# Taking the low-part subtraction of every fourth weight tile from VectorE to GpSimd in a decoder-block kernel

## The chip, the cores and the metric

The kernel runs on one core of one Trainium2 chip. The metric is the device time of one execution in microseconds (us). The engines are called as in the profile: PE is TensorE, PEld its weight load, ACT ScalarE, DVE VectorE, POOL GpSimd and SP SyncE, whose queue issues nearly all DMAs.

## What is computed

One layer of a decoder block for 256 tokens of width 2048, in float32: a norm, one wide projection, a gated mixer and a block attention beside each other, an output projection, and an MLP with a squared ReLU.

```python
h = rmsnorm(x, ln_mix[l])
z = h @ w_in[l]
uv, qkv, gates = jnp.split(z, [2 * A_WIDTH, 2 * A_WIDTH + 3 * B_WIDTH], axis=-1)
y_a = spatial_gating_mixer(uv, a_v_gain[l], a_spatial[l], a_spatial_bias[l]) @ w_proj_a[l]
q, k, v = jnp.split(qkv, 3, axis=-1)
y_b = moba_mixer(q, k, v, rel_bias) @ w_proj_b[l]
g_a, g_b = jnp.split(gates, 2, axis=-1)
merged = jax.nn.sigmoid(g_a) * y_a + jax.nn.sigmoid(g_b) * y_b
x = x + merged @ w_out[l]
h = rmsnorm(x, ln_mlp[l])
x = x + jnp.square(jax.nn.relu(h @ w_up[l])) @ w_down[l]
return rmsnorm(x, ln_final)
```

The block of keys is as long as the sequence, so the attention is plain causal attention with a bias by distance (`rel_bias`).

## The kernel before, in words

Each weight matrix is cut into tiles of 512 rows by 512 columns, 1 MB each, 288 in all, used one after the other in a fixed order: 48 for keys, queries and values (in PSUM tiles `kt`, `qt`, `v`), 16 each for `gb`, `pb`, `gv`, `u`, `pa`, `ga` and `wo`, then four rounds of 16 for `up` and 16 for `dn`, the last four of them named `last`. Tiles are counted from 0 here. Four tiles in a row make one chunk of 512 output columns.

`WeightStream` brings a tile in and splits it. `load` (line 56) puts one DMA on SP's queue into a buffer `wraw`, of which there are four. `split` rounds the tile into a high part `whi` on ACT (line 72) and takes `wlo = wraw - whi` on DVE (line 73). There are three buffers for `whi` and three for `wlo`, so tile n is split into the buffers that PE has read for tile n-3. `get` issues loads five tiles ahead and splits two tiles ahead. A load into a `wraw` buffer waits until ACT and DVE have read the tile that lay there, four tiles before. The first six tiles are split in pieces; tile 3 is split in two halves of 128x1024.

For each weight block PE makes three products: high activations by `whi`, high by `wlo`, low by `whi`. In `rows` (lines 141 to 143) that is 24 matmuls of 512 columns for one tile; in `cols` (line 158) 48 matmuls of 256 columns in groups of four, the high activations by `whi` first, then the low ones by `whi`, then `wlo`.

Other work is issued between weight tiles by `tick`: the first norm (`sq`, sums of squares by three DVE additions on lines 236, 238 and 239; `ssqp`, a product on line 243; `rs_*`; then `rb1p`, line 223), the attention heads (scores `sc`, softmax in `l`, transposes `ptp` on line 316), and `bias_rows`. That makes a table of biases: a product `rvp` (line 280), a copy to `rv` on DVE (line 281), a memset of its end (line 282), and a DMA of 2048 rows of 1 KB each to DRAM, `rv_d` (line 285). `load_bias` reads it back in pieces `bt` (line 292), the first of which the first softmax needs. SP's queue is served in order, so weight loads issued behind `rv_d` follow it.

POOL makes the identity at the start and masks four small tiles `ws` (line 423). A scheduler that works with its own durations orders each engine's instructions at build time; what is issued in a program's order above may stand elsewhere in an engine's queue.

Of the kernel before, what the change touches and what calls it, by code (L numbers as in the profile page):

```python
# [12 lines left out]
F32 = mybir.dt.float32  # L13
F32R = mybir.dt.float32r
AF = mybir.ActivationFunctionType
ALU = mybir.AluOpType
AX = mybir.AxisListType

P = 128
D = 2048  # L20
T = 256
NT = T // P
KT = D // P
# [5 lines left out]
EPS = 1e-6  # L29
NEG = -1e30  # L30
SCALE = P ** -0.5
CH = 512
KG = 4
# [1 line left out]


class WeightStream:
    """Weights in tiles of KG*128 rows by CH columns, laid out as in_tiles() does, each split exactly into two float32r parts:
    w = hi + lo. Loads and splits are issued ahead of the products that use them."""

    def __init__(self, nc, pool, chunks, ahead=2, loads_ahead=5):
        self.nc, self.pool = nc, pool
# [17 lines left out]
    def split(self, pieces=None, between=None):  # L60
        j = self.n_split
        t = self.raw.pop(j)
        if j == len(self.tiles) - 1 and self.spare:
            hi, lo = self.spare
        else:
            hi = self.pool.tile([P, KG, CH], F32R, tag="whi", name=f"whi{j}", bufs=3)
            lo = self.pool.tile([P, KG, CH], F32R, tag="wlo", name=f"wlo{j}", bufs=3)
        for a, b in pieces or (((0, 2), (2, 4)) if j < 6 else ((0, KG),)):
            if between:
                between(a, b)  # L70
            s = slice(a, b)
            self.nc.scalar.activation(hi[:, s], t[:, s], AF.Copy)  # L72
            self.nc.vector.tensor_tensor(lo[:, s], t[:, s], hi[:, s].bitcast(F32), ALU.subtract)  # L73
        self.parts[j] = (hi, lo)
        self.n_split += 1

# [11 lines left out]
def block_kernel(ctx, tc, x, x_t, ln_mix, w_in, v_gain, w_sp, b_sp, w_pa, w_pb, w_out, rel_bias,  # L88
# [23 lines left out]
        chunks += [(w_up, 0, b * D + c * CH) for c in range(4)]  # L112
        chunks += [(w_down, b * D, c * CH) for c in range(4)]

# [1 line left out]
    tasks = deque()  # L116

    def tick(limit=2):
# [10 lines left out]
    stream = WeightStream(nc, wpool, chunks)  # L129

    def rows(acts, name):
        """[tokens, CH] = acts.T @ W over 2048 rows, both token tiles."""
        ps = psum.tile([P, NT, CH], F32, tag="mm", name=name, bufs=2)
        for i in range(KT // KG):
            hi, lo = stream.get()
            for kk in range(KG):
                k = i * KG + kk
                ah, al = acts(k)
                for t in range(NT):
                    s = slice(t * P, (t + 1) * P)  # L140
                    nc.tensor.matmul(ps[:, t], ah[:, s], hi[:, kk], start=k == 0, stop=False)  # L141
                    nc.tensor.matmul(ps[:, t], ah[:, s], lo[:, kk], start=False, stop=False)  # L142
                    nc.tensor.matmul(ps[:, t], al[:, s], hi[:, kk], start=False, stop=k == KT - 1)  # L143
            if i < KT // KG - 1:
                tick()
        return ps

    def cols(acts, name):
        """[CH as 4 x 128, tokens] = W.T @ acts over 2048 rows."""
        ps = psum.tile([P, CH // P, T], F32, tag="mm", name=name, bufs=2)  # L150
        for i in range(KT // KG):
            hi, lo = stream.get()
            for kk in range(KG):
                k = i * KG + kk
                ah, al = acts(k)
                for j, (w, a) in enumerate(((hi, ah), (hi, al), (lo, ah))):
                    for n in range(CH // P):
                        nc.tensor.matmul(ps[:, n], w[:, kk, n * P : (n + 1) * P], a,  # L158
                                         start=k == 0 and j == 0 and n % 2 == 0,
                                         stop=k == KT - 1 and j == 2, skip_group_check=True)  # L160
            if i < KT // KG - 1:
                tick()
        return ps

# [1 line left out]
    ident = const.tile([P, P], F32, name="ident")  # L166
    make_identity(nc, ident)
    ones = const.tile([P, P], F32, name="ones")
# [17 lines left out]
    first = [((0, 1), (1, 2), (2, 3), (3, 4))] * 2 + [((0, 2), (2, 4))] * 2  # L186
# [4 lines left out]
    hh = hold.tile([P, KT, T], F32R, tag="h", name="hh", bufs=2)  # L191
# [10 lines left out]
        split_x(k)  # L202

    def rsqrt(dst, s, n, scale=1.0):
        """dst = (scale * s + EPS) ** -0.5, the table's root refined by a Newton step."""
        v = const.tile([P, n], F32, tag="rs_v", name="rs_v", bufs=2)
        y = const.tile([P, n], F32, tag="rs_y", name="rs_y", bufs=2)
        q = const.tile([P, n], F32, tag="rs_q", name="rs_q", bufs=2)
        nc.vector.tensor_scalar(v, s, scale, EPS, op0=ALU.mult, op1=ALU.add)
        nc.scalar.activation(y, v, AF.Sqrt)  # L210
        nc.vector.reciprocal(y, y)
        nc.vector.tensor_mul(q, y, y)
        nc.vector.tensor_mul(q, q, v)
        nc.vector.tensor_scalar(q, q, -0.5, 1.5, op0=ALU.mult, op1=ALU.add)
        nc.vector.tensor_mul(dst, y, q)

    def row_of(r, name):
        """r [token, 2] on every partition as a row [*, 256]."""
        ps = psum.tile([P, T], F32, tag="tp", name=name + "p", bufs=2)
        for t in range(NT):  # L220
            dg = const.tile([P, P], F32, tag="diag", name="dg", bufs=2)
            nc.vector.tensor_scalar(dg, ident, r[:, t : t + 1], None, op0=ALU.mult)
            nc.tensor.matmul(ps[:, t * P : (t + 1) * P], ones, dg, start=True, stop=True)
        rb = const.tile([P, T], F32, tag="rb", name=name, bufs=2)
        nc.vector.tensor_copy(rb, ps)
        return rb
# [22 lines left out]
    tasks.append(first_norm())  # L249

    def split_t(dst_h, dst_l, k0, src):
        """Two transposed blocks [128, 2, 256] in PSUM -> hi and lo parts of k0, k0 + 1."""
        nc.scalar.activation(dst_h[:, k0 : k0 + 2], src, AF.Copy)
        nc.vector.tensor_tensor(dst_l[:, k0 : k0 + 2], src, dst_h[:, k0 : k0 + 2].bitcast(F32),
                                ALU.subtract)

    def transpose_pair(src, k, name):
        """Blocks k, k + 1 (of 128 columns) of src [tokens, ...] -> PSUM [128, 2, 256]."""
        tp = psum.tile([P, 2, T], F32, tag="tp", name=name, bufs=2)
        for a in range(2):  # L260
            for t in range(NT):
                nc.tensor.transpose(tp[:, a, t * P : (t + 1) * P],
                                    src[:, t, (k + a) * P : (k + a + 1) * P], ident)
        return tp

# [1 line left out]
    bh = bl = None  # L267
    with tc.tile_pool(name="attn", bufs=1) as at:
        rv = at.tile([HEADS, RV], F32, tag="pt", name="rv", bufs=2)
# [53 lines left out]
            nc.scalar.activation(bh[:, h], pv, AF.Copy)  # L323
            nc.vector.tensor_tensor(bl[:, h], pv, bh[:, h].bitcast(F32), ALU.subtract)

        hacts = lambda k: (hh[:, k], hl[:, k])  # noqa: E731

        def scale_cols(ps, name):
            dst = at.tile([P, 4, T], F32, tag=name[:2], name=name, bufs=2)
# [6 lines left out]
        for c in range(4):  # L336
# [11 lines left out]
            ps = rows(hacts, f"v{c}")  # L348
# [4 lines left out]
                tasks.append(head(c, j, qt, kt, vt, bt))  # L353
            tick()

# [1 line left out]
        m = hold.tile([P, NT, D], F32, tag="m", name="m", bufs=1)  # L357
        for c in range(4):
            ps = rows(hacts, f"gb{c}")
# [4 lines left out]
        drain()  # L364

    with tc.tile_pool(name="gmlp", bufs=1) as gp:
# [1 line left out]
        for c in range(4):  # L368
            ps = rows(lambda k: (bh[:, k], bl[:, k]), f"pb{c}")
            for t in range(NT):  # L370
                s = m[:, t, c * CH : (c + 1) * CH]
                nc.vector.tensor_tensor(s, s, ps[:, t], ALU.mult)

# [1 line left out]
        gain = gp.tile([P, GROUPS], F32, name="gain")  # L375
        nc.sync.dma_start(gain, v_gain)
        gv = gp.tile([P, NT, D], F32, tag="gv", name="gv", bufs=1)
# [62 lines left out]
            for t in range(NT):  # L440
                nc.scalar.activation(pa[:, t, c * CH : (c + 1) * CH], ps[:, t], AF.Copy)

# [1 line left out]
        mh = ab.tile([P, KT, T], F32R, tag="ab", name="mh", bufs=2)  # L444
        ml = ab.tile([P, KT, T], F32R, tag="ab", name="ml", bufs=2)

# [13 lines left out]
                nc.vector.tensor_tensor(m[:, t, s], m[:, t, s], g[:, t], ALU.add)  # L460
            tasks.append(merged(c))

# [1 line left out]
    lnp = const.tile([P, KT], F32, name="lnp")  # L464
    nc.sync.dma_start(lnp, ln_mlp)
    x1 = hold.tile([P, NT, D], F32, tag="m", name="x1", bufs=1)
# [7 lines left out]
    r2 = const.tile([P, NT], F32, name="r2")  # L474

    def add_rows(ps, t, s, sums=None):
        """x1 += ps in columns s of token tile t; sums gets the sum of the squares."""
        xs = x1[:, t, s]
        nc.vector.tensor_tensor(xs, xs, ps, ALU.add)
        if sums is not None:  # L480
            jk = const.tile([P, CH], F32, tag="junk", name="jk", bufs=2)
            nc.scalar.activation(jk[:, : s.stop - s.start], xs, AF.Square, accum_out=sums)
# [24 lines left out]

    ab_open.close()

# [1 line left out]
    mlp = ctx.enter_context(tc.tile_pool(name="mlp", bufs=1))  # L511
    lnf = mlp.tile([P, D], F32, name="lnf")
    nc.sync.dma_start(lnf, bass.AP(tensor=ln_final.tensor, offset=ln_final.offset,
# [1 line left out]
    for b in range(DFF // D):  # L515
        hid = []
        for c in range(4):
# [10 lines left out]
                nc.scalar.activation(q, v, AF.Square)  # L528
                nc.vector.tensor_tensor(tl[:, s], q, th[:, s].bitcast(F32), ALU.subtract)
            hid.append((th, tl))  # L530
        acts = lambda k: (hid[k // 4][0][:, k % 4], hid[k // 4][1][:, k % 4])  # noqa: E731
        last = b == DFF // D - 1
        for c in range(3 if last else 4):
            ps = rows(acts, f"dn{b}_{c}")
# [5 lines left out]
                else:  # L540
                    add_rows(ps[:, t], t, s)

# [1 line left out]
    spare = [hold.tile([P, KG, CH], F32R, tag="h", name=f"spare{i}", bufs=2) for i in range(2)]  # L544
    stream.spare = tuple(spare)
    out_v = out.rearrange("(t p) d -> t p d", p=P)
# [42 lines left out]


def in_tiles(w):
    """[rows, cols] as [row tile, column tile, 128, KG, CH]: each weight tile in one piece."""
    r, c = w.shape
    return np.asarray(w).reshape(r // (KG * P), KG, P, c // CH, CH).transpose(0, 3, 2, 1, 4)


def _onehot():
    """Which bucket a distance of 255 - m falls in, for m < 256; the rest is masked."""
    n = np.arange(256)
    half = BUCKETS // 2  # L600
    large = half + (np.log(np.maximum(n, 1).astype(np.float32) / np.float32(half))
# [45 lines left out]
```

## Time and profile before

| | |
|---|---|
| runs, median | 1664.79 us (two runs: 1663.89 and 1665.68) |
| span of the profiled execution, first to last instruction | 1662.5 us |
| median less span, taken as what lies around it | 2.3 us |
| PE busy | 1651.6 us, 99% |
| DVE busy | 850.9 us, 51% |
| ACT busy | 688.8 us, 41% |
| POOL busy | 4.3 us |
| mean granted PE clock | 0.998 |
| DMA | 317.16 MB, mean 191 GB/s |

The page gives the span of the profiled execution and no other time for it, so its own time is read as the span and the 2.3 us around it. A row of a timeline is start, duration, engine, line, operation, names; in brackets stands the idle time of the engine before it and what ended it.

### The profile page before, as it was taken

To read this page: it belongs to the slowest core of one execution; us is meant where nothing else is said; L and a number is where in the kernel's file an instruction comes from. 1 tells how busy PE (TensorE), PEld (TensorE's weight loads), DVE (VectorE), ACT (ScalarE), POOL (GpSimd) and SP (SyncE) were. 2 spreads that over 40 slices of the span, in tenths; PEclk is the share of its full clock that TensorE was granted. 3 is DMA by queue.
4 is the path that set the end of the run, shared out by engine and by line. 5 is a ranking of instruction groups with operands and counts; after the bars stand their busy time and mean duration, and the time that the engine had idled before them with its cause. 6 is when DMAs were issued, how large, how long until landed. Compare 5 with 4: busy or idle time off the path is not lost.

```text
span 1662.5 us, 22670 instructions
## 1 busy us (share of the span) xinstructions
PE 1651.6 (99%) x9988; PEld 1483.7 (89%) x9988; DVE 850.9 (51%) x726; ACT 688.8 (41%) x614; POOL 4.3 (0%) x11
## 2 busy tenths in 40 slices
PE   9999999999999999999999999999999999999997
PEld 9899999888888899888888999889988998899986
DVE  7545544544445555544555555444545455445554
ACT  7444343443334443434444444334443443334432
POOL 0000000000000000000000000000000000000000
PEclk9999999999999999999999999999999999999999
DMA  9855444465555554555465554555555555555551
GB/s 317 254 193 187 165 178 170 159 223 185 200 192 189 192 199 169 184 191 202 178 234 189 210 178 178 202 189 191 178 186 194 190 190 178 201 181 186 190 183 74
DMA packets 51762, 317.16 MB, mean 191 GB/s; under 512 B 5664, under 2 KB 10832, under 8 KB 14928
## 3 DMA queue, kind: packets, MB, share of 16 engines
q1 hardware_dynamic: 51632, 315.71, 53.9%
q8 instruction: 78, 1.28, 0.3%
q14 instruction: 20, 0.16, 0.0%
q0 software_dynamic: 32, 0.01, 0.0%
HBM read 311.50 MB, written 4.19 MB: 190 GB/s over the span
## 4 chain that ended last, share of the span: by engine, by line
PE 99%; DMA 0%; DVE 0%; ACT 0%; issue 0%; DVEq 0%; POOL 0%; POOLq 0%; ACTq 0%
PE up L158 22%; PE dn L142 7%; PE dn L143 7%; PE dn L141 7%; PE kt L158 6%; PE qt L158 6%; PE u L158 6%; PE v L142 2%; PE wo L143 2%; PE ga L143 2%; PE gb L141 2%; PE wo L141 2%; PE ga L141 2%; PE wo L142 2%; PE pa L141 2%; PE v L141 2%
## 5 line engine op out<-in xcount | busy, mean ns | idle before, releaser
L73 DVE TENSOR_TENSOR wlo<-wraw,whi 128x2048 fp32r<-128x2048 f32 (+2 forms) x297 | 658.9, 2219 | 644.8 <-ACT whi L72 644.8
L72 ACT ACTIVATE whi<-wraw 128x2048 fp32r<-128x2048 f32 (+2 forms) x297 | 551.5, 1858 | 832.6 <-PE up L158 188.9
L141 PE MATMUL dn<-whi,hh 128*128 128x512 f32 x480 | 186.8, 389 | 0.0
L142 PE MATMUL dn<-wlo,hh 128*128 128x512 f32 x480 | 186.8, 389 | 0.0
L143 PE MATMUL dn<-whi,hl 128*128 128x512 f32 x480 | 186.7, 389 | 0.0
L158 PE MATMUL up<-h2h,whi 128*128 128x256 f32 x1024 | 164.7, 283 | 0.0
L158 PE MATMUL up<-h2l,whi 128*128 128x256 f32 x1024 | 164.6, 283 | 0.0
L158 PE MATMUL up<-h2h,wlo 128*128 128x256 f32 x1024 | 164.6, 283 | 0.0
L158 PEld LDWEIGHTS up<-h2h,whi 128*128 128x128 f32 x1024 | 141.5, 192 | 0.3
L158 PEld LDWEIGHTS up<-h2h,wlo 128*128 128x128 f32 x1024 | 141.3, 192 | 0.0
L158 PEld LDWEIGHTS up<-h2l,whi 128*128 128x128 f32 x1024 | 141.3, 192 | 0.0
L143 PEld LDWEIGHTS dn<-whi,hl 128*128 128x128 f32 x480 | 90.1, 188 | 18.7
L141 PEld LDWEIGHTS dn<-whi,hh 128*128 128x128 f32 x480 | 90.1, 188 | 18.6
L142 PEld LDWEIGHTS dn<-wlo,hh 128*128 128x128 f32 x480 | 90.1, 188 | 18.6
L141 PE MATMUL gb<-whi,hh 128*128 128x512 f32 x128 | 50.6, 395 | 0.0
L141 PE MATMUL wo<-whi,mh 128*128 128x512 f32 x128 | 50.6, 395 | 0.0
L141 PE MATMUL ga<-whi,hh 128*128 128x512 f32 x128 | 50.4, 394 | 0.0
L141 PE MATMUL v<-whi,hh 128*128 128x512 f32 x128 | 50.0, 391 | 0.0
L141 PE MATMUL pa<-whi,ah 128*128 128x512 f32 x128 | 50.0, 391 | 0.0
L143 PE MATMUL wo<-whi,ml 128*128 128x512 f32 x128 | 50.0, 390 | 0.0
L142 PE MATMUL v<-wlo,hh 128*128 128x512 f32 x128 | 50.0, 390 | 0.0
L143 PE MATMUL ga<-whi,hl 128*128 128x512 f32 x128 | 49.9, 390 | 0.0
(180 smaller groups left out, 2394.8 us busy)
## 6 DMA issues: line engine op xcount, KB each, us to landing
wraw<-in_w_in SPq DMA_DIRECT2D x108, 1024.0 KB, 4.8
wraw<-in_w_up SPq DMA_DIRECT2D x64, 1024.0 KB, 4.8
wraw<-in_w_down SPq DMA_DIRECT2D x64, 1024.0 KB, 4.8
wraw<-in_w_pb SPq DMA_DIRECT2D x16, 1024.0 KB, 4.8
wraw<-in_w_pa SPq DMA_DIRECT2D x16, 1024.0 KB, 4.8
wraw<-in_w_out SPq DMA_DIRECT2D x16, 1024.0 KB, 4.8
wraw<-in_w_in SPq DMA_DIRECT2D x8, 256.0 KB, 4.7
wraw<-in_w_in SPq DMA_DIRECT2D x4, 512.0 KB, 7.5
```

The costliest lines, as they stand in the source:

```text
L72: self.nc.scalar.activation(hi[:, s], t[:, s], AF.Copy)
L73: self.nc.vector.tensor_tensor(lo[:, s], t[:, s], hi[:, s].bitcast(F32), ALU.subtract)
L141: nc.tensor.matmul(ps[:, t], ah[:, s], hi[:, kk], start=k == 0, stop=False)
L142: nc.tensor.matmul(ps[:, t], ah[:, s], lo[:, kk], start=False, stop=False)
L143: nc.tensor.matmul(ps[:, t], al[:, s], hi[:, kk], start=False, stop=k == KT - 1)
L158: nc.tensor.matmul(ps[:, n], w[:, kk, n * P : (n + 1) * P], a, start=k == 0 and j == 0 and n % 2 == 0, stop=k == KT - 1 and j == 2, skip_g ...
```

## The change

For tiles with a number of remainder 3 by 4 (3, 7, ..., 287: 72 tiles, 73 instructions, since tile 3 is split in halves) the subtraction goes to POOL. All other instructions stay, and all sizes and buffers. One line is added, so line numbers of the changed kernel are one higher from line 74 on.

```diff
             s = slice(a, b)
             self.nc.scalar.activation(hi[:, s], t[:, s], AF.Copy)
-            self.nc.vector.tensor_tensor(lo[:, s], t[:, s], hi[:, s].bitcast(F32), ALU.subtract)
+            eng = self.nc.gpsimd if j % 4 == 3 else self.nc.vector
+            eng.tensor_tensor(lo[:, s], t[:, s], hi[:, s].bitcast(F32), ALU.subtract)
```

The scheduler also orders some other work anew, all of it in the first six tiles. On PE, before, the bias product `rvp` stands inside tile 3 (`wlo_252` and `whi_251` are tile 3's parts, `_315` and `_316` tile 4's):

```order
L158 MATMUL kt_196<-hh,whi_251 128x256 x4
L158 MATMUL kt_196<-hl,whi_251 128x256 x4
L280 MATMUL rvp<-oh,rbs 16x384
L158 MATMUL kt_196<-hh,wlo_252 128x256 x4
L158 MATMUL kt_196<-hh,whi_251 128x256 x4
L158 MATMUL kt_196<-hl,whi_251 128x256 x4
L158 MATMUL kt_196<-hh,wlo_252 128x256 x4
L158 MATMUL qt_445<-hh,whi_315 128x256 x4
```

After, from the middle of tile 4 into tile 5 (`whi_372`):

```order
L159 MATMUL qt_445<-hh,whi_315 128x256 x4
L159 MATMUL qt_445<-hl,whi_315 128x256 x4
L159 MATMUL qt_445<-hh,wlo_316 128x256 x4
L281 MATMUL rvp<-oh,rbs 16x384
L224 MATMUL rb1p<-dg,ones 128x128 x2
L159 MATMUL qt_445<-hh,whi_372 128x256 x4
```

So `rvp` moved from inside tile 3 to the end of tile 4, right ahead of `rb1p`; `ssqp`, which stood inside tile 4, now stands between tiles 3 and 4. The rest of PE's order is as it was.

On DVE, before, the copy and the memset of `rv` stand among the splits of tiles 3 to 5 (`wlo_252`, `wlo_316`, `wlo_373`):

```order
L236 TENSOR_TENSOR sq<-sq 128x2048
L73 TENSOR_TENSOR wlo_252<-wraw_121,whi_251 128x1024
L238 TENSOR_TENSOR sq<-sq 128x1024
L281 COPY rv<-rvp 16x384
L73 TENSOR_TENSOR wlo_316<-wraw_197,whi_315 128x1024 x2
L239 TENSOR_TENSOR sq<-sq 128x512
L282 MEMSET rv 16x128
L73 TENSOR_TENSOR wlo_373<-wraw_199,whi_372 128x1024 x2
```

After, from the diagonal for `rb1p` on, past tile 6's split (`wlo_449`):

```order
L223 TENSOR_SCALAR dg<-ident,r_186 128x128 x2
L282 COPY rv<-rvp 16x384
L74 TENSOR_TENSOR wlo_449<-wraw_249,whi_448 128x2048
L226 COPY rb_507<-rb1p 128x256
L283 MEMSET rv 16x128
L333 TENSOR_TENSOR kt_676<-kt_196,rb_507 128x512 x2
```

The copy now follows tile 5's split and the whole of the norm's small steps, and the memset follows tile 6's split and the copy of `rb`. SP's order of DMAs has not changed: `rv_d` stands behind the load of tile 9 and ahead of that of tile 10. On POOL the 73 subtractions stand in order of tiles; two of the four masks stand between those of tiles 55 and 59, the others ahead of tiles 107 and 111.

## Rows read from the trace of the kernel before

**Rows 1.** The page, part 1: busy us, share of the span, instructions
```profile
PE 1651.6 (99%) x9988; PEld 1483.7 (89%) x9988; DVE 850.9 (51%) x726; ACT 688.8 (41%) x614; POOL 4.3 (0%) x11
```

**Rows 2.** The page, part 5: the subtraction on DVE (busy, mean ns; idle before)
```profile
L73 DVE TENSOR_TENSOR wlo<-wraw,whi 128x2048 fp32r<-128x2048 f32 (+2 forms) x297 | 658.9, 2219 | 644.8 <-ACT whi L72 644.8
```

**Rows 3.** Groups of POOL, by line: busy us, mean ns; idle before
```profile
L423 POOL TENSOR_SCALAR_AFFINE_SELECT ws<-ws 128x512 f32<-128x512 f32 x4 | 2.9, 731 | 627.6 <-DMA ws<-in_w_sp 627.6
```

**Rows 4.** Timeline of ACT, DVE and PE: tile 279 split and used
```profile
1593.26 1.92 ACT L72 ACTIVATE whi<-wraw 128x2048 fp32r<-128x2048 f32 x1 [2.35 <-issue]
...
1595.21 2.29 DVE L73 TENSOR_TENSOR wlo<-wraw,whi 128x2048 fp32r<-128x2048 f32 x1 [1.99 <-ACT whi L72]
...
1604.12 0.39 PE L142 MATMUL dn<-wlo,hh 128*128 128x512 f32 x1
```

**Rows 5.** Timeline of ACT: tile 3's two halves
```profile
20.92 1.06 ACT L72 ACTIVATE whi<-wraw 128x1024 fp32r<-128x1024 f32 x1 [0.27 <-DMA wraw<-in_w_in]
...
23.20 1.04 ACT L72 ACTIVATE whi<-wraw 128x1024 fp32r<-128x1024 f32 x1
```

**Rows 6.** Timeline of PE: tile 3, the bias product, tiles 4 and 5
```profile
24.28 0.64 PE L158 MATMUL kt<-hh,wlo 128*128 128x256 f32 x4
...
27.25 0.81 PE L280 MATMUL rvp<-oh,rbs 32*16 32x384 f32 x2
27.99 0.74 PE L158 MATMUL kt<-hh,wlo 128*128 128x256 f32 x4
...
30.01 0.64 PE L158 MATMUL qt<-hh,whi 128*128 128x256 f32 x4
...
36.66 0.64 PE L158 MATMUL qt<-hh,whi 128*128 128x256 f32 x4
```

**Rows 7.** Timeline of DVE, 22 to 32 us
```profile
23.95 2.28 DVE L236 TENSOR_TENSOR sq<-sq 128x2048 f32<-128x2048 f32 x1
...
28.42 0.54 DVE L281 COPY rv<-rvp 16x384 f32<-16x384 f32 x1
...
31.81 0.17 DVE L282 MEMSET rv<- 16x128 f32 x1
```

**Rows 8.** Timeline of SP: issue of the bias table and what stands beside it
```profile
34.21 0.33 SPq L56 DMA_DIRECT2D wraw<-in_w_in  x1
34.59 0.69 SPq L285 DMA_DIRECT2D rv_d<-rv  x1
...
60.13 0.39 SPq L292 DMA_DIRECT2D bt<-rv_d  x1
```

**Rows 9.** DMA issues: KB each, us from issue to landing
```profile
wraw<-in_w_in SPq DMA_DIRECT2D x108, 1024.0 KB, 4.8
...
gain<-in_v_gain SPq DMA_DIRECT2D x1, 8.0 KB, 2.1
```

**Rows 10.** Windows, core 0: busy time by engine, clock, DMA share, GB/s
```profile
39.00:58.00 19.00, 19.00 (x146) 18.38 (x146) 9.25 (x8) 3.83 (x2) 0.00 (x0) 1.00 0.85 106
```

**Rows 11.** Timeline: tiles 10 and 11 split (ACT, DVE) and used (PEld, PE)
```profile
62.69 1.92 ACT L72 ACTIVATE whi<-wraw 128x2048 fp32r<-128x2048 f32 x1 [12.45 <-DMA wraw<-in_w_in]
65.16 1.91 ACT L72 ACTIVATE whi<-wraw 128x2048 fp32r<-128x2048 f32 x1 [0.55 <-DMA wraw<-in_w_in]
...
64.64 2.29 DVE L73 TENSOR_TENSOR wlo<-wraw,whi 128x2048 fp32r<-128x2048 f32 x1 [8.78 <-ACT whi L72]
...
66.98 0.19 PEld L142 LDWEIGHTS v<-wlo,hh 128*128 128x128 f32 x1 [0.42 <-DVE wlo L73]
...
72.55 0.39 PE L142 MATMUL v<-wlo,hh 128*128 128x512 f32 x1
```

**Rows 12.** Timeline: softmax of heads 4 and 5, the next split, the transposes
```profile
156.50 1.01 DVE L312 TENSOR_SCALAR l<-l,st 128x128 f32<-128x128 f32 x4
159.58 2.29 DVE L73 TENSOR_TENSOR wlo<-wraw,whi 128x2048 fp32r<-128x2048 f32 x1 [2.07 <-ACT whi L72]
...
157.87 0.82 PE L316 MATMUL ptp<-ident,l 128*128 128x128 f32 x6
```

## The prediction, made before the changed kernel was run

> **What bounds the kernel now.** I read the page's busy times first. PE is busy for 1651.6 of 1662.5 us [rows 1], so a change pays only where it touches PE, and costs only where PE comes to wait. DVE is at 51%, and the subtraction that is moved is most of that: 658.9 us in 297 instructions, ahead of which DVE stood idle for another 644.8 us, waiting for ACT [rows 2]. An engine that waits so much for its input is not the bound. Taking a quarter of its work away frees about 72 x 2.29 = 165 us of DVE, and none of PE.
>
> The second view is the timeline of one tile in the long regular part. For tile 279, a tile that moves, ACT ends `whi` at 1593.26 + 1.92 = 1595.18, DVE subtracts from 1595.21 to 1597.50, and PE's first product with that `wlo` stands at 1604.12 [rows 4]. The reader is to see a deadline here: from the end of `whi` PE gives the subtraction 8.94 us, and DVE needs 2.29. That repeats from tile to tile, since each split begins when PE leaves the tile three before it, and so has about two tiles of PE's work to hide behind.
>
> The third view is the start, where such reserves are missing. Tile 3 needs the first half of its `wlo` at 24.28 [rows 6], and ACT ends that half of `whi` at 20.92 + 1.06 = 21.98 [rows 5]: 2.3 us. Tile 10 has no reserve at all: ACT stood idle for 12.45 us until its load had landed, DVE ended at 64.64 + 2.29 = 66.93, and PE waited 0.42 us for that [rows 11]. The load was late since it is queued on SP behind the table of biases. That table was issued at 34.59, and the read of it, which waits for it, came at 60.13 [rows 8]. From 39 to 58 us the DMA engines were busy for 0.85 of the time at only 106 GB/s [rows 10]: 19 us x 106 GB/s is 2 MB, which is the table. So whatever makes the table later makes PE later, one for one, at tile 10.
>
> **The change, part by part.** *The subtraction on POOL.* Nothing in the trace is a subtraction on POOL. From below it cannot be quicker than DVE's 2.29 us by any row here. From above, a mask of 128x512 takes 0.73 us [rows 3], which is 2.9 us for 2048 columns with one operand; with two operands read one after the other it is 5.9 us. I take 4.4, half-way from the one-operand time to that end, and keep 2.3 and 5.9. All of these meet the 8.94 us, so in the regular part the cost is nothing; the cover is PE's work on the two tiles ahead. If POOL took T, the cost would be T - 8.94 for each of some 71 tiles. Tile 11 is tighter: `whi` ends at 65.16 + 1.91 = 67.07 and PE uses `wlo` at 72.55 [rows 11], 5.48 us; the upper end would cost 0.4 us there, my value nothing.
>
> A price is on a page of the Trainium skill, "GPSIMD Engine Reference", section 3.1: 4497 ns for this operation on 2048 float32 columns, against 2293 on VectorE. The trace has 2.29 for VectorE; no run yet shows the other. By that figure too, the sum is the same.
>
> The next load into the buffer now waits for POOL, some 2 us later than for DVE. A load takes 4.8 us [rows 9] and has about two tiles' time in hand; no cost. POOL's queue is in order, so a mask that waits for its DMA holds up the subtractions behind it; but in the program's order the DMAs of the two masks ahead of tile 59 stand on SP directly behind that tile's own load, so that they land a few us after it, and its `whi` is not made much sooner. I count nothing.
>
> *Tile 3.* Half a tile is 2.2 us by my value, 1.15 to 2.9 by the ends. The first half runs from 22.0 to 24.2, in time for 24.28; the second from 24.24 (`whi` ends at 23.20 + 1.04, rows 5) to 26.4, and PE wants it six groups of 0.48 us after 24.28, at 27.16. Cost 0, at the upper end 0.7. Before, tile 3 ran from 23.32 to 30.01 [rows 6], 6.69 us for 12 x 0.48 = 5.76 of products and 0.81 at most of `rvp`, so that 0.1 to 0.4 us was waiting; that goes. I count -0.2.
>
> *The bias table, moved.* This is the term that counts. `rvp` now stands behind tile 4. Tile 3 ends at 23.32 + 5.76 = 29.08. `ssqp` costs 0.9 (tile 4 took 36.66 - 30.01 = 6.65 with it, rows 6) and has its sums in time, since DVE, rid of tile 3, can start them at 23.95 and has 2.28 us and two shorter additions to do [rows 7]. Tile 4 then ends at 29.98 + 5.76 = 35.7 and `rvp` at 36.5. The copy takes 0.54 [rows 7]: 37.1. Behind it DVE does tile 6's split, 2.29: 39.4; then the copy of `rb`, taken as 0.5; then the memset, 0.17: 40.1. So SP issues the table at 40.1 in place of 34.59, 5.5 us later.
>
> Not all of that reaches tile 10. Before, the load of tile 9 was issued at 34.21 [rows 8] and lands 4.8 us later, at 39.0, so the table, queued behind it, could hardly move earlier. After, the queue is empty when the table is issued, and its data begins within the 2.1 us that a small DMA needs to land [rows 9]: between 40.1 and 42.2. The delay is therefore 1.1 to 3.2 us, and 5.5 if the whole of the issue carries over. [...] Tile 10's load and `whi` come 2.7 us later, and PE, which had no reserve there, waits 3.1 us instead of 0.4. Tile 11's load, its subtraction and its deadline move together. Nothing later can give the time back: PE's idle time is 1662.5 - 1651.6 = 10.9 us in all [rows 1], nearly all of it before the first product and after the last.
>
> *Sum.* -0.2 + 0 + 2.7 = +2.5 us on the span of 1662.5, so 1665.0, and with 2.3 around it 1667.3. The median of the runs before is that span and the 2.3, 1664.79.
>
> **Rivals.** *POOL misses the deadline (slower).* At T = 9.4 the loss is 71 x 0.46 = 33 us, which is 2%; at T = 12 it is 71 x 3.06 = 217 us, 1882 us in all. For it: no row shows POOL with two operands or with this output type. Against it: the masks give 5.9 at most. It decides from 8.94 us.
>
> *DVE and POOL exclude each other.* If an instruction on one held up the other while both read, it would bite in tile 3. POOL's halves would hold the instructions ahead of the three additions on DVE (two short ones for `hl`, under 1 us) and then the additions themselves: these would begin not at 23.95 but when POOL's second half is through, 26.4 to 27.3 by who goes first, and take 4.2 (2.28 and, by their columns, about 1.2 and 0.7). I take the later, 31.5. `ssqp`, first in line on PE at 29.1, would wait 2.4 us, and the table's chain with it: +4.9 in all, 1669.7. "SBUF — State Buffer" of the Trainium skill, section "Who interferes with whom", says just this: a VectorE instruction with two SBUF inputs and a GpSimd instruction that reads SBUF take turns, whole instruction by whole instruction. No row here shows it, since POOL did nothing beside DVE. In the regular part the deadline covers it. The softmax is where it could hurt: for heads 4 and 5 DVE ends at 156.50 + 1.01 = 157.51 and PE's transposes stand at 157.87 [rows 12], 0.36 us. But tile 27's subtraction came only at 159.58 [rows 12], and in the timelines of the other pairs I found no moved tile between scores and transposes that would hold them up; even 2.3 us at each of eight pairs would be 18 us, about 1%.
>
> *The late table costs nothing.* If its data was held up before by something that now falls away, PE loses nothing and gains the 0.2: 1664.6. For it: before, the table was ready at 31.98 and waited on SP until 34.59. Against it: the chain by DVE to 40.1 lies past 39.0 whatever the queue does.
>
> *A gain by a freed DVE* would need waits of PE to remove, and within the stream of products there is next to none: 0.4 us at tile 10 and 0.1 to 0.4 at tile 3, as above.
>
> **How the numbers follow.** The forecast has 0.66, exclusion 0.16, a free table 0.12, a POOL past the deadline 0.05, a gain of 2% 0.01. A measurement of this kernel tells about 2%, 33 us, from no change. All cases but the last two lie within it, so faster 0.01, same 0.94, slower 0.05. The predicted time is 1667.3. Its own range is 1665.7 (delay 1.1) to 1670.1 (delay 5.5). The range goes down to the free table, 1664.0, and up past exclusion, 1671.0; POOL past the deadline is left out.
>
> **What would show it right or wrong.** Right: subtractions on POOL of 4 to 5 us; no PE wait on POOL after tile 11; the table issued near 40 us; PE's wait at tile 10 near 3 us; DVE near 686 us busy, PE's busy time as before. Exclusion: a DVE subtraction or addition that begins only when POOL ends, or lasts much longer than 2.29, and `ssqp` waiting for DVE. It would be wrong if PE waited on `wlo` in every fourth tile, if the granted clock fell after the wait at tile 10, or if the table's later issue did not move tile 10's load.

## The result, and the profile after

The changed kernel takes 1677.11 us (median of two runs, 1676.30 and 1677.91), 12.3 us more than before; the ratio is 1.0073 with a 95% interval of 1.0054 to 1.0092. The forecast was 1667.3 with a range up to 1671.0: the sign is right, the size is not. The profiled execution spans 1674.6 us, 12.1 more than before. Below, "after" is this kernel; its line numbers are one higher from line 74 on.

The page of after, its busy times and the two groups of the subtraction (columns as in [rows 1] and [rows 2]):

```profile
PE 1655.9 (99%) x9988; PEld 1485.9 (89%) x9988; DVE 717.3 (43%) x653; ACT 688.6 (41%) x614; POOL 339.0 (20%) x84
...
L74 DVE TENSOR_TENSOR wlo<-wraw,whi 128x2048 fp32r<-128x2048 f32 (+2 forms) x225 | 500.9, 2227 | 756.0 <-ACT whi L72 755.9
L74 POOL TENSOR_TENSOR wlo<-wraw,whi 128x2048 fp32r<-128x2048 f32 (+1 forms) x72 | 330.1, 4586 | 1275.3 <-ACT whi L72 1267.1
```

POOL takes 4.6 us where DVE took 2.29, and DVE is relieved of 133.6 us, not of 165. The waits of PE say where the loss is not (what waits, for what; total us, times, longest):

```profile
PE v L142 <- ACT whi L72: 3.3, 1, 3.3
PE ssqp L244 <- DVE sq L240: 1.9, 1, 1.9
PE last L575 <- DVE wlo L74: 1.5, 2, 1.2
PE v L143 <- DVE wlo L74: 1.5, 1, 1.5
```

No row has PE waiting for POOL. These waits lie at tile 4 (`ssqp`), tile 10 (`v`) and in the last chunk, and the two further rows of this view, 1.1 and 0.5 us, at the first products; so the regular part lost nothing. I set the start of every weight tile on PE in after against before, from the two timelines. The difference is 0.5 at tiles 1 to 3 (a later first load), 2.6 at tile 4, 8.1 at tile 10's first product with `wlo`, 9.9 at tile 11, the same 9.9 at every tile from there to 284, and 12.05 from tile 287 to the end.

**Tile 3 and the table.** The timelines of POOL, DVE, PE and SP in after, one fence for each engine (start, us, engine, line, operation):

```profile
22.20 4.96 POOL L74 TENSOR_TENSOR wlo<-wraw,whi 128x1024 fp32r<-128x1024 f32 x2 [19.79 <-ACT whi L72]
```

```profile
22.55 4.89 DVE L197 SCALAR_TENSOR_TENSOR hl<-xt,lnm,hh 128x256 fp32r<-128x256 f32 x2 [0.65 <-ACT hh L196]
27.36 2.28 DVE L237 TENSOR_TENSOR sq<-sq 128x2048 f32<-128x2048 f32 x1
...
30.94 0.69 DVE L240 TENSOR_TENSOR sq<-sq 128x512 f32<-128x512 f32 x1
...
42.43 0.17 DVE L283 MEMSET rv<- 16x128 f32 x1
```

```profile
31.68 1.05 PE L244 MATMUL ssqp<-ones,sq 128*128 128x1 f32 x8 [1.94 <-DVE sq L240]
```

```profile
42.62 0.69 SPq L286 DMA_DIRECT2D rv_d<-rv  x1
...
67.20 0.39 SPq L293 DMA_DIRECT2D bt<-rv_d  x1
```

Two short instructions for `hl`, which last 0.87 us before, last 4.89 us here: they run over POOL's two halves, which end at 22.20 + 4.96 = 27.16. The first addition begins at 27.36, not at 23.95 [rows 7], the last ends at 31.63, and `ssqp` waits for it. The chain behind it ends with the memset of `rv`, so the table is issued at 42.62 in place of 34.59 [rows 8], 8.0 us later, and read 7.1 later. Of the 8.0, 0.5 is the later first load and 1.9 PE's wait for `ssqp`; the 5.6 left are near the 5.5 that the forecast worked out for the scheduler's new order alone.

**Tile 10.** The windows of after around it (PE, PEld, DVE, ACT, POOL busy; granted clock, DMA share, GB/s):

```profile
68.00:70.00 2.00, 1.47 (x9) 1.01 (x7) 0.00 (x0) 0.00 (x0) 0.00 (x0) 1.00 1.00 418
70.00:72.00 2.00, 0.00 (x0) 0.00 (x0) 0.00 (x0) 1.21 (x1) 0.00 (x0) 1.00 1.01 422
72.00:74.00 2.00, 0.80 (x1) 0.29 (x1) 1.27 (x1) 1.42 (x2) 0.00 (x0) 0.53 0.99 408
...
76.00:78.00 2.00, 2.00 (x6) 1.51 (x5) 0.73 (x3) 1.98 (x2) 2.00 (x1) 0.50 1.02 411
78.00:80.00 2.00, 2.00 (x9) 1.58 (x8) 2.00 (x1) 1.03 (x1) 1.86 (x1) 0.76 0.93 385
```

The reader sees the wait (3.3 and 1.5 us of idle PE) and then its second price: the granted clock falls to 0.50, the 1.2 GHz level, while PE stands, and stays there to about 79 us. From its first `wlo` product to tile 11, tile 10 took 82.23 - 75.08 = 7.15 us, before 72.32 - 66.98 = 5.34: 1.8 us more.

**The end.** ACT, POOL, DVE and PE in after (`spare` is tile 287; DVE's row of 5.02 us is tile 285):

```profile
1636.45 1.92 ACT L72 ACTIVATE spare<-wraw 128x2048 fp32r<-128x2048 f32 x1 [4.16 <-DMA wraw<-in_w_down]
```

```profile
1638.45 4.63 POOL L74 TENSOR_TENSOR spare<-wraw,spare 128x2048 fp32r<-128x2048 f32 x1 [6.85 <-ACT spare L72]
```

```profile
1640.20 5.02 DVE L74 TENSOR_TENSOR wlo<-wraw,whi 128x2048 fp32r<-128x2048 f32 x1 [5.58 <-ACT whi L72]
```

```profile
1645.28 0.50 PE L575 MATMUL last<-wlo,hh 128*128 128x512 f32 x1 [1.17 <-DVE wlo L74]
```

The scheduler splits the last tile ahead of tile 285. DVE's subtraction for 285 begins while POOL works on 287, and lasts 2.7 us longer than its 2.29.

### The profile page after: what moved, and what is told of

Read it like the earlier page. It is cut to its first block, busy times and chain, and to the rows that moved or that the text cites. A ratio compares the mean times of both kernels' runs of the same rounds, so it can differ in the third digit from the quotient of the medians.

```text
span 1674.6 us, 22697 instructions
## 1 busy us (share of the span) xinstructions
PE 1655.9 (99%) x9988; PEld 1485.9 (89%) x9988; DVE 717.3 (43%) x653; ACT 688.6 (41%) x614; POOL 339.0 (20%) x84
## 4 chain that ended last, share of the span: by engine, by line
PE 95%; DMA 2%; DVE 1%; ACT 1%; issue 0%; SPq 0%; DVEq 0%; ACTq 0%
PE up L159 22%; PE dn L142 6%; PE dn L143 6%; PE dn L144 6%; PE u L159 5%; PE qt L159 5%; PE kt L159 4%; DMA wraw<-in_w_in 2%; PE wo L144 2%; PE ga L144 2%; PE gb L142 2%; PE wo L142 2%; PE pa L142 2%; PE wo L143 2%; PE ga L142 2%; PE ga L143 2%
## 5 line engine op out<-in xcount | busy, mean ns | idle before, releaser
L74 DVE TENSOR_TENSOR wlo<-wraw,whi 128x2048 fp32r<-128x2048 f32 (+2 forms) x225 | 500.9, 2227 | 756.0 <-ACT whi L72 755.9
L74 POOL TENSOR_TENSOR wlo<-wraw,whi 128x2048 fp32r<-128x2048 f32 (+1 forms) x72 | 330.1, 4586 | 1275.3 <-ACT whi L72 1267.1
L144 PE MATMUL v<-whi,hl 128*128 128x512 f32 x128 | 50.5, 395 | 0.0
```

The costliest lines, as they stand in the source:

```text
L74: eng.tensor_tensor(lo[:, s], t[:, s], hi[:, s].bitcast(F32), ALU.subtract)
```

## The experiments

The theory after this reading: DVE and POOL take turns; this costs at tile 3 and, through the table and the clock, at tile 10, and at the end; the regular part costs nothing. Where a diff shows only the condition, the rest is the changed kernel.

**1. Only the regular part**

```diff
-            eng = self.nc.gpsimd if j % 4 == 3 else self.nc.vector
+            eng = self.nc.gpsimd if j % 4 == 3 and 11 <= j < 287 else self.nc.vector
```

> GpSimd subtracts only for tiles 11, 15, ..., 283 (69 tiles); tiles 3, 7 and 287 stay on VectorE. Theory (the loss of 12.3 us sits at tile 3, at tile 10 by way of the bias table, and at the last tile): nothing is left to lose, 1664.8 us and within 0.5 of it, with GpSimd's subtractions still at a mean near 4.6 us and some of VectorE's longer than 2.3. Rival (the loss is spread over the regular part, 0.17 us for each tile moved): 1676 us.

Measured: 1664.78 us, ratio 1.0003 [0.9995, 1.0012]. 69 subtractions on POOL, mean 4.62 us, cost nothing within that interval; the loss is in the moves of tiles 3, 7 and 287.

**2. Only tile 3** (`j == 3`)

> GpSimd subtracts only for tile 3, in its two halves. Theory: 2.7 us ahead of tile 5 (the sums of squares wait for GpSimd's halves, and ssqp for them) and 7.2 us more at tile 10, by which the table is late, the fall of the granted clock there included: 1664.8 + 9.9 = 1674.7 us. Rival (the loss is spread over all moved tiles): 1665 us. Rival (turn-taking costs its 2.7 us, and the wait at tile 10 is made by tile 7's subtraction on GpSimd, not by the table): 1667.5 us.

Measured: 1674.90 us, ratio 1.0061 [1.0048, 1.0074]. One tile of 288, in two instructions, makes 10.6 of the 12.3 us. PE waits 1.97 us for `ssqp`, the table is issued at 43.85, and tile 10 waits 2.94 and 1.82 us, with tile 7 on DVE. So the rival with tile 7 falls.

**3. The table early, with all moved tiles**

```diff
         def bias_rows():
-            for _ in range(4):
+            for _ in range(2):
                 yield
...
+            for _ in range(2):
+                yield
             nc.sync.dma_start(rv_d, skew)
```

> The changed kernel, with the bias product, its copy and the memset issued two steps sooner, the table's DMA where it was. The table can then be issued as soon as tile 9's load is, near 36.6 us in place of 42.6. Theory (the whole delay of the issue carries over to tile 10): PE's wait at tile 10 falls below 1 us, the granted clock stays at full speed there, and what is left is 2.7 us at tile 3 and 2.1 at the end: 1669.6 us. Rival (the table is not what makes tile 10 late): 1677 us, with the wait at tile 10 as before this edit.

Measured: 1668.72 us, ratio 1.0028 [1.0017, 1.0038]. The table was issued at 36.67, PE's wait at tile 10 is 0.34 us and the clock there 1.00. 8.4 us are gone against after, and 4.4 us over the kernel before are left.

**4. The table late, with nothing on POOL** (the kernel before)

```diff
-            nc.vector.memset(rv[:, 256:], NEG)
+            nc.vector.tensor_scalar(rv[:, 256:], r1[:HEADS, :1].to_broadcast([HEADS, P]), 0.0, NEG,
+                                    op0=ALU.mult, op1=ALU.add)
```

> The kernel before, with all subtractions on VectorE and the same order on every queue; the end of rv is set from r1 in place of a memset, so that the table is issued near 38.2 us in place of 34.6, 3.6 us later. Theory (the whole delay carries over, whatever the queue does): tile 10's load lands 3.6 us later and PE loses 3.5, 1668.3 us, more only if the granted clock falls. The prediction's own step (the table stands behind tile 9's load until 39.0 anyway, and its data starts within 2.1 us of its issue): 0 to 1.3 us, 1664.8 to 1666.1.

Measured: 1669.74 us, ratio 1.0030 [1.0018, 1.0042], +5.4 us and so beyond both, nearer to the theory with a clock that falls: the windows show 0.50 from 72 to 74 us. This profiled execution had its first tiles 1.9 us later (tile 1 at 13.70 in place of 11.80), as had those of experiments 1 and 3; the table's issue is at 39.57.

Nine profiles settle it without such offsets. For each: when SP issues `rv_d`, when PE starts its first product with tile 10's `wlo`, and the time between (us):

| kernel | `rv_d` issued | first `wlo` product of tile 10 | between |
|---|---|---|---|
| before | 34.59 | 66.98 | 32.39 |
| tiles 283 and 287 (7, below) | 34.61 | 67.93 | 33.32 |
| tile 3, table early (8, below) | 36.08 | 68.65 | 32.57 |
| regular part (1) | 36.24 | 68.79 | 32.55 |
| table early (3) | 36.67 | 69.12 | 32.45 |
| table late, POOL idle (4) | 39.57 | 71.79 | 32.22 |
| after | 42.62 | 75.08 | 32.46 |
| tile 3 alone (2) | 43.85 | 75.96 | 32.11 |
| after, a second profile (9, below) | 45.19 | 77.54 | 32.35 |

Over 10.6 us of issue time the distance holds within 1.2 us: the whole of the issue's delay arrives at tile 10. The four other profiles (5, 6 and the first of 7) have 32.1 to 33.1.

How it arrives is in the trace's record of DMA packets, where the table's have 1 KB and a load's 8 KB. Before, the table's first packet starts at 38.35, 3.76 us after the issue, as the last packets of tile 9's load start (38.89): the load did hold it up, as the forecast said. After, the load is through, and the first packet starts at 43.95, 1.33 us after the issue. The table's data so begins 5.6 us later, not 8.0. The rest is lost in its first microseconds. Before, 38 to 42 us:

```profile
38.00:39.00 1.00, 1.00 (x11) 1.00 (x10) 0.62 (x1) 0.34 (x1) 0.00 (x0) 1.00 0.86 321
39.00:40.00 1.00, 1.00 (x10) 1.00 (x10) 1.00 (x1) 0.00 (x0) 0.00 (x0) 1.00 1.00 265
40.00:41.00 1.00, 1.00 (x11) 1.00 (x10) 0.67 (x1) 0.00 (x0) 0.00 (x0) 1.00 0.87 98
41.00:42.00 1.00, 1.00 (x10) 1.00 (x10) 0.83 (x2) 0.00 (x0) 0.00 (x0) 1.00 0.85 94
```

After, 43 to 46 us:

```profile
43.00:44.00 1.00, 1.00 (x10) 1.00 (x10) 0.78 (x2) 0.00 (x0) 1.00 (x1) 1.00 0.03 5
44.00:45.00 1.00, 1.00 (x11) 1.00 (x10) 0.00 (x0) 0.00 (x0) 1.00 (x1) 1.00 0.87 99
45.00:46.00 1.00, 1.00 (x11) 1.00 (x10) 0.00 (x0) 0.71 (x1) 1.00 (x1) 1.00 0.86 91
```

Behind the load the table starts quickly: 332 of its 2048 packets have started by 40 us, at 265 GB/s in the last of these microseconds, and then it goes on at 94 to 98. Alone it has 91 to 99 GB/s from the start.

The first packet of tile 10's load stands 19.6 us behind the table's first before, and 21.9 after; it comes 7.9 us later (57.92 and 65.80). All 13 profiles fall into these two groups: nine where the table waits behind a load (3.7 to 4.0 us from issue to first packet, 17.3 to 19.7 from there to tile 10's load), and four where the load is through by then (1.33 and 21.9). Experiment 4 shows it without POOL, beside experiment 1, which had the same later first load: the issue is 3.3 us later, the table's first packet 1.0, tile 10's load 3.2, its `wlo` product 3.0. Why the table starts quicker behind a load, no run shows.

**5. Both engines on every tile at once: turn-taking measured**

```diff
+            for e, c in ((self.nc.vector, slice(a, b)),) if not 11 <= j < 284 else (
+                    (self.nc.vector, slice(0, 2)), (self.nc.gpsimd, slice(2, 4))):
+                e.tensor_tensor(lo[:, c], t[:, c], hi[:, c].bitcast(F32), ALU.subtract)
```

> Every tile from 11 to 283 is cut in two halves of 128x1024, one for VectorE and one for GpSimd at the same moment. If the two do not exclude each other, VectorE's halves take 1.2 us and GpSimd's 2.5, as in tile 3. If they take turns, instruction by instruction, the two of one tile take 1.2 + 2.5 = 3.7 us together: the one that comes second shows its wait in its own duration, VectorE's near 3.6 us where GpSimd goes first, or GpSimd's near 3.6 where VectorE does. The time is 1664.8 us by both, since a tile has 8.9 us from whi to its first product with wlo.

Measured: 1665.75 us, ratio 1.0008 [0.9999, 1.0017]. POOL and DVE of one tile, and POOL's group:

```profile
1193.18 3.44 POOL L75 TENSOR_TENSOR wlo<-wraw,whi 128x1024 fp32r<-128x1024 f32 x1 [2.31 <-ACT whi L72]
...
L75 POOL TENSOR_TENSOR wlo<-wraw,whi 128x1024 fp32r<-128x1024 f32 x273 | 926.8, 3395 | 686.1 <-ACT whi L72 682.6 <-DVE l L303 3.4
```

```profile
1193.13 1.23 DVE L75 TENSOR_TENSOR wlo<-wraw,whi 128x1024 fp32r<-128x1024 f32 x1 [1.12 <-ACT whi L72]
```

DVE, 0.05 us ahead, runs at its own 1.23 us; POOL's half ends 2.26 us after DVE's, at a recorded length of 3.44. 262 of its 273 instructions read 3.4 or 3.5. In six pairs POOL started first, by 0.12 us: there POOL reads 2.40 and DVE 3.36. In the other five POOL's half met none of DVE's halves at its start, and reads 2.40 too. The two exclude each other for the whole instruction, whoever starts first goes first, and the wait of the second stands inside its own duration.

"SBUF — State Buffer" of the Trainium skill, section "Who interferes with whom", says of a VectorE instruction with two SBUF inputs that it contends with a GpSimd instruction that reads SBUF, and calls that contention an exclusive lock; the trace agrees, with 3.44 us against 2.40.

**6. Every tile of the regular part on POOL; the deadline.** Two kernels: `11 <= j < 284` as the condition, and a second with every POOL subtraction of the regular part done twice.

> GpSimd subtracts for every tile from 11 to 283, VectorE for none of them. Theory (4.6 us meet both the deadline of 8.94 and PE's 5.76 us a tile; VectorE's instructions of the softmax and the norms wait for GpSimd now and then, but have cover): 1665 to 1670 us. Rival (turn-taking with the softmax, the norms and the other steps on VectorE that PE waits for is not covered): over 1675 us, with PE waiting for ACT and DVE behind instructions of VectorE that last some 5 us. Rival (GpSimd in a row is slower than alone in one of four): over 1700 us.

Measured: 1678.90 us, ratio 1.0077 [1.0063, 1.0091]. POOL met every deadline (273 instructions, mean 4.63 us). What was lost was DVE's work, as the rival had it. DVE and the softmax around 76 us:

```profile
72.94 8.36 DVE L313 TENSOR_SCALAR l<-l,st 128x128 f32<-128x128 f32 x2
81.22 0.15 DVE L311 RECIPROCAL st<-st 128x2 f32<-128x2 f32 x1
81.41 9.08 DVE L313 TENSOR_SCALAR l<-l,st 128x128 f32<-128x128 f32 x2
...
L313 DVE TENSOR_SCALAR l<-l,st 128x128 f32<-128x128 f32 x16 | 34.8, 2177 | 0.5
L526 DVE SCALAR_TENSOR_TENSOR v<-up,rb 128x512 f32<-128x512 f32 x32 | 20.6, 686 | 262.7 <-PE up L159 262.7
L530 DVE TENSOR_TENSOR hl<-q,hh 128x512 fp32r<-128x512 f32 x32 | 76.6, 2431 | 20.2 <-ACT q L529 20.2
```

PE's transposes `ptp` wait five times for that scaling, 8.9 us in all, and by 88 us the clock is at 0.50. The groups also say which instructions take turns: `hl`, two operands in SBUF, lasts 2431 ns in the mean in place of 684; the scaling `l`, 128x128 with one tensor operand, 2177 in place of 284; `v`, which reads PSUM and SBUF, 686 in both, although 16 of its 32 instructions overlap a subtraction on POOL (691 to 693 each).

> GpSimd subtracts for tiles 11, 15, ..., 283 and does each subtraction twice into the same place (the second repeats the first); tiles 3, 7, 287 stay on VectorE. This measures the deadline. Theory (8.94 us from the end of whi): 2 x 4.6 = 9.2 us miss it by 0.26, 69 times, 18 us: 1683 us, with PE waiting for GpSimd in nearly every fourth tile. Rival (VectorE's subtractions cut in between the two and make it 11.5): 69 x 2.56 = 177 us, 1842 us. Rival (the deadline gives way, since whi comes earlier where its buffer allows): 1665 us.

Measured: 1700.51 us, ratio 1.0212 [1.0196, 1.0227], between the theory and the first rival. POOL needs 9.29 us for the two in the regular part. Each of 32 tiles in `rows` then has its first `wlo` product 0.44 us late and the next tile another 0.17. That puts the deadline near 9.29 - 0.44 = 8.85 us against the 8.94 of [rows 4]. Tiles in `cols` lose nothing: there `wlo` is used third in each group and later. 8.0 us come at tile 11, where DVE cut in and POOL needed 11.14, and some 6 at the end. So the deadline was right for `rows`; my price counted all 69 tiles and none of the edges.

**7. The end: tile 287 alone, and tiles 283 and 287** (`j == 287`; `j in (283, 287)`)

> GpSimd subtracts only for the last tile, 287. Theory (turn-taking again: VectorE's subtraction for tile 285 is ready while GpSimd works on tile 287's, ahead of its turn, and comes 2 us late): 1664.8 + 2.1 = 1666.9 us, with VectorE's subtraction of tile 285 near 5 us long and PE waiting for it. Rival (the lateness at the end follows from the 9.9 us lost before, by the loads): 1664.8 us and no wait there.

Measured: 1664.82 us, ratio 0.9999 [0.9990, 1.0008]: the theory as it was then is wrong. DVE's subtraction of tile 285 does last 5.02 us there, but PE waits only 0.15 us. Start of `spare` on ACT and DVE's tile 285 in that kernel:

```profile
1626.64 1.92 ACT L72 ACTIVATE spare<-wraw 128x2048 fp32r<-128x2048 f32 x1 [2.47 <-DMA wraw<-in_w_down]
```

```profile
1630.39 5.02 DVE L74 TENSOR_TENSOR wlo<-wraw,whi 128x2048 fp32r<-128x2048 f32 x1 [3.90 <-ACT whi L72]
```

ACT waits 2.47 us for the load there and 4.16 in after. The load of tile 287 goes into the buffer of tile 283, which POOL reads 2.3 us longer than DVE does. In experiment 1 this lateness was there (4.25) without cost, since DVE needs 2.3 us for `spare`. So both together, as the next theory:

> GpSimd subtracts only for tiles 283 and 287. Theory (two causes that hurt together: GpSimd reads tile 283's buffer 2.3 us longer, so that the load of tile 287 into it comes later, and GpSimd's subtraction for 287 then holds up VectorE's for 285): each alone cost nothing that could be measured, the two together cost 2.1 us, 1666.9 us, with ACT waiting some 4.2 us for tile 287's load and PE 1.2 us for VectorE at tile 285. Rival (the lateness at the end is that of the start, carried along): 1664.8 us.

Measured: 1667.31 us, ratio 1.0012 [1.0003, 1.0022], +2.6 us: each alone costs nothing, both cost 2 to 2.6.

**8. Turn-taking at tile 3 without the late table** (`j == 3`, with experiment 3's edit)

> GpSimd subtracts only for tile 3, and the bias product, its copy and the memset come two steps sooner. Theory (turn-taking at tile 3 by itself costs what PE waits for ssqp and the table's issue at 36.6 in place of 34.6): 1.9 to 2.7 us, 1667 us, the granted clock at full speed at tile 10. With the 2.1 us of the end it then makes up the 4.4 us that were left with all moved tiles. Rival (turn-taking at tile 3 costs nothing by itself, only by the table): 1664.8 us.

Measured: 1667.02 us, ratio 1.0011 [1.0002, 1.0020], +2.3 us, with the clock at 1.00 at tile 10. This and the end's 2.6 are 4.9 us, near the 4.4 left in experiment 3. Experiments 2 and 8 both move tile 3 alone and differ only in how early the table's steps stand in the program: 10.6 us and 2.3. So most of what tile 3 costs needs the late table, which is in the main the scheduler's new order; turn-taking adds to its lateness and costs 2.3 us by itself. The early table without POOL was not run.

**9. The changed kernel once more**

> The changed kernel once more, beside the others on one chip. Theory: the parts add up, 2.2 us (tile 3) + 7.5 (table at tile 10, with the clock) + 2.1 (end) = 11.8 us over the kernel before, 1676.6 us.

Measured: 1678.77 us, ratio 1.0079 [1.0065, 1.0093], the parts' sum and 2 us, within the spread of its runs (1676.3 to 1680.7). The profile shows one source of that spread: here, and in experiment 2, the wait for `ssqp` was also followed by the lower clock:

```profile
30.00:32.00 2.00, 0.77 (x6) 0.77 (x6) 1.97 (x3) 1.03 (x1) 0.00 (x0) 0.92 0.58 238
32.00:34.00 2.00, 2.00 (x10) 2.00 (x10) 2.00 (x4) 0.45 (x2) 0.00 (x0) 0.50 0.05 12
```

In after's first profile, with a wait just as long, it stayed at 1.00.

No version beat the kernel before; that of experiment 1 equals it.

## Why the prediction was wrong

- *What bounds the kernel; the regular part at no cost; T = 4.4 with a deadline of 8.94.* Right: 4.61 us in the regular part, 8.85 as the deadline by experiment 6, nothing lost in 69 tiles. The page "GPSIMD Engine Reference" of the Trainium skill, section 3.1, was near with 4497 ns, which it gives for an addition.
- *"DVE, rid of tile 3, can start them at 23.95".* Failed: it started them at 27.36. Turn-taking was a rival at 0.16 and is what happened. Its mechanism was worked out rightly (last addition ends at 31.5, measured 31.63; wait 2.4, measured 1.94; table 5.5 + 2.4 = 7.9 us later, measured 8.0). Its weight was wrong: "no row here shows it" was taken as a reason for a small chance, though POOL had done nothing beside DVE, so that no row could show it. The -0.2 of tile 3 beside it is too small to tell here.
- *"Not all of that reaches tile 10": 2.7 of 5.5 us.* Failed, and the largest of the mis-sized terms: the whole arrives, in every profile. Its first half was right: before, the load of tile 9 held the table until 38.35 (39.0 in the forecast). No run shows the 2.7. After, the data began 1.33 us after the issue, inside the 2.1 allowed; with that the step would have come to 40.1 + 1.33 - 38.35 = 3.1. What it left out is the time from the table's first packet to tile 10's load, taken as the same in both: it is 19.6 us before and 21.9 after, and the 2.3 us between them make the 3.1 into 5.4 of 5.5. The prediction's third view had said "one for one", and that is what came. The rival's price carried the same error: 1669.7 by the 2.7, 1672.5 with the whole 5.5. The upper end named in this step, "5.5 if the whole of the issue carries over", was the right one.
- *The granted clock.* Its fall was named among what would make the forecast wrong, and priced at nothing: 1.8 us in after at tile 10.
- *"Nothing later can give the time back", and nothing later adds any.* The first half held. The second was not looked at for the last tiles, where the scheduler splits tile 287 ahead of 285 and the deadline I took from tile 279 doesn't hold: 2.1 us.
- *Sum.* 8.1 at tile 10, 1.8 of clock and 2.1 at the end make 12.0; the span grew by 12.1. Of the 8.1, 0.5 are the later first load.
- *DVE near 686 us.* It was 717.3: some 30 us of waiting for POOL stand in its durations (`sg` 18.2 in place of 5.5, `gv` 6.9 for 2.6, `hl` 11.4 for 7.3, `al` 9.4 for 5.5, two `wlo` 4.6 more).

## What to carry to other kernels

Work that GpSimd does with operands in SBUF isn't beside VectorE's work of the kinds measured here but between it: price its duration as a delay of the VectorE instruction that starts meanwhile, at each place where that one has no reserve, the first and the last tiles above all. Then look at what the scheduler does with the rest: one tile of 288 cost 10.6 us with the order that it made, and 2.3 with the table's steps issued earlier. Leaving out the tiles at both ends (experiment 1) brings the loss to nothing, but no gain either, as VectorE wasn't the bound. In this kernel the delay of a long DMA's issue reached the load queued behind it whole. That its data had to wait for the queue anyway is no reason to count less, until the time that it then needs to move is compared too.

## What the runs showed of the hardware that was not expected

A wait for the other engine is recorded as duration, not as idle time: 4.89 us for two instructions of 0.48, 5.02 for one of 2.29. Instructions with one tensor operand can take turns too (the softmax's scaling, 2177 ns for 284), while `v`, which reads PSUM beside SBUF, did not lengthen (686 in both). A 2 MB table of 1 KB rows, issued behind a 1 MB load on the same queue, began beside that load's last packets, 3.7 to 4.0 us after its issue, and moved at 265 GB/s in its second microsecond (before) and then at 94 to 98; where the load was through, it began 1.33 us after its issue and moved at 91 to 99 GB/s from the start (after). PE's wait at tile 10 in after, 4.8 us in two pieces, was followed by a granted clock of 0.50 until 79 us; a wait of 1.9 us for `ssqp`, and then its eight products of one column (1.05 us), were followed by it in two of the three profiles that had them.
